# Eight of the 24 gates of each mixer by seven block products ahead of the attention, and the sink as a column of the summed row

## The chip, the cores and the metric

The kernel runs on one core of a Trainium2 chip, in one launch. The metric is the device time in microseconds (us). Three runs of the kernel before gave 2394.09, 2394.22 and 2396.0 us. A core has engines that run their own instruction lists and wait for each other by semaphores: TensorE (PE, matrix products into PSUM banks), VectorE (DVE), ScalarE (ACT), GpSimd (POOL), and SyncE (SP), which here only issues DMAs. ScalarE and POOL issue DMAs too. A DMA's issue waits in the list of the engine that issues it.

## The reference

A trunk of two layers over 512 tokens of width 1024, in float32. Each layer is a half-step feed-forward, a mixer, and a second half-step feed-forward. The mixer is what changes:

```python
h = rms_norm(x, norm_g[l, 1])
proj = h @ w_in[l]
qa, ka, va, qd, kd, vd, qc, kc, vc = jnp.split(proj, PROJ_OFFSETS, axis=-1)
...
g = jax.nn.sigmoid(h @ w_gate[l] + b_gate[l]).reshape(B, S, N_BRANCHES, D_MODEL)
merged = (g[:, :, 0] * (ya @ w_branch[l, 0])
          + g[:, :, 1] * (yb @ w_branch[l, 1])
          + g[:, :, 2] * (yc @ w_branch[l, 2]))
x = x + merged @ w_o[l]
```

Here `ya` is the neighbourhood attention (8 heads on a grid of 8 x 64 tokens), `yb` the differential attention (4 heads with two softmax maps each) and `yc` the windowed attention (8 query heads, 2 key heads). So there are three gates of width 1024. In tiles of 128 output columns they are 24 gates, named (branch, tile): (0, 0) to (2, 7). In the windowed attention the softmax has one more logit, the sink of its head, which has no value behind it:

```python
sink_l = jnp.broadcast_to(sink.astype(jnp.float32).reshape(Hkv, G, 1, 1), logits.shape[:-1] + (1,))
p = jax.nn.softmax(jnp.concatenate([logits, sink_l], axis=-1), axis=-1)[..., :-1]
```

## The kernel before

Activations lie transposed: eight tiles `h` of 128 features by 512 tokens. A float32 product is made of three products of reduced operands: each matrix is split into a high part (a cast on ScalarE, `whi`, line 100) and a low part (a subtraction on VectorE, `wlo`, line 101), and TensorE sums hi x hi, hi x lo and lo x hi (lines 122, 123 and 125). A **direct gate** is one weight tile of 1024 columns: 8 x 3 = 24 matmuls of 512 columns, then a multiplication by the norm (`z`, line 1583) and a tanh on ScalarE. The results stay in SBUF until the merge of their branch.

The feed-forward has another way, class `Seven` (its matmuls are on line 889). It takes two output tiles at a time, as a 2 x 2 block product in seven block products instead of eight, by sums and differences of the blocks. The activations' sums are class `Sides`, made once per feed-forward (VectorE lines 699 to 709 and the low halves on line 720). The weights' sums are made by DMAs that add, partly in DRAM long before. A tile of Seven needs several split weights: `wa` (the first raw tile), `w31` (a sum loaded as `wsum`), `w24`, and the corner `w22` from `a22`. A stage that is not prepared in DRAM uses the order `WIDE_FIRST` with 72 matmuls a tile, 12 of 512 columns and 60 of 256.

In the mixer, `qk(0)` computes the first queries and keys, and `v_stacked` (lines 1276, 1277 and 1280) the values of the neighbourhood attention: four weight tiles, each with 24 matmuls of 512, into four PSUM banks that stay open until the last weight. The banks are emptied by `vn` on ScalarE (line 1302) and VectorE (line 1303). The three attentions then run as generators. `beside(attention, steps, n)` sets a list of other products (queries, keys, gates, merges) between the eight steps of each attention stage, so that TensorE has work while a softmax is under way. There are four stages of each attention: na, diff and gqa.

Raw weights come by SP's queue into `raw`, three buffers: a load is issued when the buffer's last reader is done, and SP's loads go out in their order. `ahead_by` (line 789) issues a few of the DMAs that prepare the next feed-forward after each weight, as many as `PACE` says.

The sink in the windowed attention: the row of 256 or 384 scores is lifted by its bias on VectorE, which also gives the row's bound `negm`; ScalarE makes the exponentials and their sum `tot`; one more exponential of a single column gives the sink's share `se` (line 1571), which VectorE adds to `tot` (line 1572).

## Time and profile before

| | before |
|---|---|
| three runs, us | 2394.09, 2394.22, 2396.0 |
| the profiled execution's own time, us | 2394.87 |
| its span on the core, us | 2393.1 |
| mixer 0, from its first q product to the output product, us of the span | about 352 to 865 |
| mixer 1 stands behind mixer 0 by, us | 1181.1 |

The span leaves out what lies around the core's first and last instruction, 1.8 us here. All times of instructions are counted from the span's start. In the group rows "out<-in" names the tiles without their numbers, and "x24" is a count of instructions. In the chain of work that ended last each piece stands with its start and length; in the timeline a bracket at the end says how long the engine stood idle before the instruction, and who released it.

### The profile page before, as it was taken

How to read it: one execution, taken by the hardware profiler on the slowest of the kernel's cores; microseconds unless marked ns; L12 is line 12 of the kernel's file. 1: busy time of each engine (PE TensorE's matmuls, PEld its weight loads, DVE VectorE, ACT ScalarE, POOL GpSimd, SP SyncE). 2: the span in 40 equal slices, each digit the busy share in tenths (PEclk: the TensorE clock that was granted, in tenths of full speed). 3: DMA queues.
4: the chain of work that ended last, by engine and by line, in shares of the span. 5: the costliest groups of instructions: out<-in, count | busy, mean ns of one | idle time of the engine just before them, and what ended most of it. 6: DMA issues, size and time to landing. Idle time of an engine off the chain costs nothing.

```text
span 2393.1 us, 35725 instructions
## 1 busy us (share of the span) xinstructions
PE 2377.4 (99%) x12954; PEld 2047.3 (86%) x12954; DVE 1834.6 (77%) x3328; ACT 1380.0 (58%) x2551; POOL 369.3 (15%) x524
## 2 busy tenths in 40 slices
PE   9999999999999999999999999999999999999998
PEld 7999888888888888888888888888888888888887
DVE  6999885766667679997899997767666666899832
ACT  5565545756566446664456664467566574566632
POOL 3100024412131100110201011333212100000000
PEclk9999999999999999999999999999999999999999
DMA  7665787655698647886858887766556624455532
GB/s 200 182 185 163 248 243 211 172 157 136 193 221 250 190 147 232 266 257 200 233 185 240 272 268 234 215 170 167 144 140 168 157 95 132 163 190 189 172 114 71
DMA packets 149776, 452.92 MB, mean 189 GB/s; under 512 B 18264, under 2 KB 23688, under 8 KB 148640
## 3 DMA queue, kind: packets, MB, share of 16 engines
q1 hardware_dynamic: 89856, 278.50, 34.5%
q0 software_dynamic: 40352, 107.36, 22.6%
q10 hardware_dynamic: 19392, 64.78, 7.5%
q8 instruction: 102, 1.67, 0.3%
q14 instruction: 74, 0.61, 0.1%
HBM read 428.52 MB, written 138.44 MB: 237 GB/s over the span
## 4 chain that ended last, share of the span: by engine, by line
PE 95%; DVE 2%; ACT 1%; issue 1%; DMA 1%; SPq 0%; POOLq 0%; POOL 0%; ACTq 0%; DVEq 0%
PE mm L889 18%; PE plain L395 10%; PE mm L125 9%; PE pr L889 9%; PE mm L123 9%; PE mm L122 9%; PE pv L889 4%; PE mm L395 3%; PE av L1382 2%; PE mm L1600 2%; PE mm L1595 2%; PE mm L1596 2%; PE t L1372 1%; PE s L1327 1%; PE s L1328 1%; PE av L1484 1%
## 5 line engine op out<-in xcount | busy, mean ns | idle before, releaser
L101 DVE TENSOR_TENSOR wlo<-raw,whi 128x1024 fp32r<-128x1024 f32 x234 | 278.8, 1196 | 111.5 <-ACT whi L100 91.0
L100 ACT CAST whi<-raw 128x1024 fp32r<-128x1024 f32 x234 | 238.6, 1027 | 211.3 <-PE mm L123 76.6
L122 PE MATMUL mm<-h,whi 128*128 128x512 f32 x800 | 318.7, 398 | 0.0
L123 PE MATMUL mm<-h,whi 128*128 128x512 f32 x800 | 313.7, 392 | 0.0
L125 PE MATMUL mm<-h,wlo 128*128 128x512 f32 x800 | 197.8, 389 | 0.6 <-DVE wlo L101 0.6
L109 DVE TENSOR_TENSOR wlo<-raw,whi 128x1024 fp32r<-128x1024 f32 x156 | 184.2, 1218 | 6.0 <-ACT whi L108 5.9
L125 PEld LDWEIGHTS mm<-h,wlo 128*128 128x128 f32 x800 | 150.1, 188 | 32.3 <-DVE wlo L101 1.0
L123 PEld LDWEIGHTS mm<-h,whi 128*128 128x128 f32 x800 | 150.5, 188 | 28.8
L122 PEld LDWEIGHTS mm<-h,whi 128*128 128x128 f32 x800 | 150.4, 188 | 28.4
L108 ACT CAST whi<-raw 128x1024 fp32r<-128x1024 f32 x156 | 156.8, 1051 | 10.2 <-DMA raw<-in_w_gu 8.6
L395 PE MATMUL plain<-g,whi 128*128 128x512 f32 x672 | 160.7, 389 | 0.0
L395 PEld LDWEIGHTS plain<-g,whi 128*128 128x128 f32 x672 | 126.1, 188 | 26.3
L761 POOL DMA_DIRECT2D d_odd<-in_w_gu x60 | 51.6, 859 | 516.1 <-DVE gu L925 254.6
L1341 ACT ACTIVATE lg<-lg,negm 128x256 f32<-128x256 f32 (+1 forms) x192 | 114.0, 594 | 29.0 <-DVE negm L1338 23.2
L1009 ACT COPY gu<-mm 128x512 f32<-128x512 f32 (+1 forms) x78 | 41.9, 538 | 131.2 <-PE mm L889 131.2
L108 ACT CAST whi<-wsum 128x1024 fp32r<-128x1024 f32 x90 | 94.8, 1053 | 39.3 <-PE pv L889 32.7
L109 DVE TENSOR_TENSOR wlo<-wsum,whi 128x1024 fp32r<-128x1024 f32 x90 | 109.5, 1217 | 5.5 <-PE plain L395 3.2
L925 DVE TENSOR_TENSOR gu<-pr,gu 128x256 f32<-128x256 f32 x234 | 98.2, 420 | 8.6 <-ACT gu L963 4.4
L1583 DVE TENSOR_TENSOR z<-mm,rb 128x512 f32<-128x512 f32 x48 | 33.2, 691 | 81.7 <-PE mm L125 81.6
L889 PEld LDWEIGHTS mm<-h,whi 128*128 128x128 f32 x624 | 83.7, 189 | 5.6 <-PE st L250 0.4
L1222 DVE SCALAR_TENSOR_TENSOR qn<-mm,rb 128x512 f32<-128x512 f32 x44 | 34.8, 794 | 68.1 <-PE mm L125 68.1
L889 PE MATMUL mm<-h,whi 128*128 128x256 f32 x624 | 86.9, 281 | 0.0
(367 smaller groups left out, 6185.3 us busy)
## 6 DMA issues: line engine op xcount, KB each, us to landing
raw<-in_w_gu SPq DMA_DIRECT2D x94, 512.0 KB, 4.4
d_odd<-in_w_gu ACTq DMA_DIRECT2D x60, 512.0 KB, 7.2
d_even<-in_w_gu ACTq DMA_DIRECT2D x60, 512.0 KB, 6.0
d_odd<-in_w_gu POOLq DMA_DIRECT2D x60, 512.0 KB, 8.4
wsum<-d_odd SPq DMA_DIRECT2D x60, 512.0 KB, 3.6
raw<-d_even SPq DMA_DIRECT2D x60, 512.0 KB, 4.6
raw<-in_w_gate SPq DMA_DIRECT2D x48, 512.0 KB, 5.0
raw<-in_w_qk SPq DMA_DIRECT2D x44, 512.0 KB, 3.9
```

The source lines that it names most:

```text
L100: nc.scalar.copy(hi[:, w], raw[:, w])
L101: lower[:] = [nc.vector.tensor_tensor(out=lo[:, w], in0=raw[:, w], in1=f(hi[:, w]), op=ALU.subtract).ins]
L108: nc.scalar.copy(hi, src)
L109: nc.vector.tensor_tensor(out=lo, in0=src, in1=f(hi), op=ALU.subtract)
L122: nc.tensor.matmul(ps, wh, xhi[k], start=k == 0, stop=False)
L123: nc.tensor.matmul(ps, wh, xlo[k], start=False, stop=False)
L125: nc.tensor.matmul(ps, wl, xhi[k], start=False, stop=k == n - 1)
L395: nc.tensor.matmul(ps, w, x, start=start, stop=stop, skip_group_check=True)
L761: dma = nc.gpsimd.dma_start(out, more, accum_op=ALU.add, max_dma_last_dim=4 * 1024)
L889: nc.tensor.matmul(out, wk, bk, start=go, stop=end, skip_group_check=True)
L925: nc.vector.tensor_tensor(out=out, in0=in0, in1=in1, op=ALU.add)
L1341: nc.scalar.activation(p, p, AF.Exp, bias=negm, scale=-1.0, accum_out=total)
```

## The change

In each mixer eight gates, (0, 2) to (0, 7), (1, 0) and (1, 1), are computed as four tiles of a new class `Gates`, which is `Seven` with another source, other buffers and another end. The four tiles run between `v_stacked` and the first attention stage. Their sides (class `MixedSides`) are made while `v_stacked` runs, one after each of its weights. A result goes through its tanh and is stored to DRAM from POOL's queue; the merge that needs it loads it again on SP's queue. The gates (1, 2) to (1, 7) are still direct products beside the attention, and they go to DRAM and back too, from their `z` buffer. The gates (0, 0), (0, 1) and those of branch 2 stay as they were, in SBUF.

The lists beside the attention lose the eight gates. The four na stages and the second diff stage have as many products as before; diff 0, 1 and 3 and gqa 0, 2 and 3 have one fewer, gqa 1 two fewer. `PACE["mixer"]` is raised, as there are fewer weights to pace by. In the windowed attention POOL copies the sink's negative into the column behind the row of scores, and the one exponential sums that column too; `se` and its addition are gone.

```diff
-    "mixer": ((1, 1, 2.5), (0.6, 1, 1.8)),
+    "mixer": ((1.2, 2, 2.5), (0.7, 1.4, 1.8)),
...
+    AHEAD = ((0, 1), (0, 2), (0, 3), (1, 0))
+
+    class MixedSides(Sides):
+        def whole_room(self, mp):
+            return mp.tile([P, S], F32, tag="gate", name="xf", bufs=3)
...
+        def kept(self, mp, one, t3):
+            self.t = [mp.tile([P, 2, H], F32R, tag="yp", name="side", bufs=12) for _ in range(3)]
+            for src, out in zip((one[:, 0], one[:, 1], t3), self.t):
+                self.halves(src, out)
...
+    class Gates(Seven):
...
+        def total(self, m):
+            t = self.fp.tile([P, 2, S], F32, tag="pt", name="wsum", bufs=4)
+            nc.sync.dma_start(t, self.source(m).rearrange("n p c -> p n c")[:, :, 0:S])
+            t = t.rearrange("p n c -> p (n c)")
+            nc.gpsimd.dma_start(t, self.source(m)[1], accum_op=ALU.add)
+            return t
+        def scratch(self):
+            return self.fp.tile([P, 5, H], F32, tag="pt", name="gu", bufs=4)
...
+            def opened(t, odd):
+                c = i * KC + 2 * n + odd
+                nc.scalar.activation(t, t, AF.Tanh, bias=self.bg[:, c : c + 1], scale=0.5)
+                self.stored(i, 2 * n + odd, t)
...
-                        p = l_tile()[:, :w]
-                        softmax(p, ps, reversed_view(bias, 383 - u, [[1, w]]), nsink[:, head : head + 1], negm[:, j : j + 1], tot[:, j : j + 1])
-                        se = small.tile([P, 1], F32, tag="se", name="se")
-                        nc.scalar.activation(se, negm[:, j : j + 1], AF.Exp, bias=sink[:, head : head + 1])
-                        nc.vector.tensor_tensor(out=tot[:, j : j + 1], in0=tot[:, j : j + 1], in1=se, op=ALU.add)
+                        full = l_tile()
+                        p = full[:, :w]
+                        nc.gpsimd.tensor_copy(out=full[:, w : w + 1], in_=nsink[:, head : head + 1])
+                        softmax(p, ps, reversed_view(bias, 383 - u, [[1, w]]), nsink[:, head : head + 1], negm[:, j : j + 1], tot[:, j : j + 1], full[:, : w + 1])
...
+            def stored(i, m, t):
+                gates[i, m] = dram.tile([P, S], F32, tag=f"d_gate{l}{i}{m}", name="d_gate")
+                nc.gpsimd.dma_start(gates[i, m], t)
...
+                if i < 2 and (i, mm) != (0, 0):
+                    for m in (2 * mm, 2 * mm + 1):
+                        if mm % 2:
+                            t = work.tile([P, S], F32, tag="x", name="gate", bufs=2)
+                        else:
+                            t = mp.tile([P, S], F32, tag="gate", name="gate", bufs=3)
+                        nc.sync.dma_start(t, gates[i, m])
...
-            run([qk(0), v_stacked()])
-            beside(attend_na(0), [qk(1), *g0(0)], 3)
+            outset = (x for g in (qk(0), v_stacked()) for x in g)
+            sides = []
+            next(outset)
+            for c in range(4):
+                next(outset)
+                sides.append(MixedSides(mp, h, c, [None] * KC))
+            run([outset])
+            tiles = Gates(l, h, mp, sides, bg, stored)
+            tiles.fetch(0)
+            tiles.wa[0] = parted(tiles.raw[0])
+            tiles.fetch_a22(0)
+            tiles.fetch(1)
+            with tc.issue_after(sides[3].mark):
+                tiles.w31[0] = parted(tiles.sums[0])
+            for m in range(tiles.end):
+                tiles.tile(m)
+            with tiles.in_order():
+                tiles.flush()
+            beside(attend_na(0), [qk(1), gate(0, 0)], 3)
...
-            beside(attend_gqa(2), [merge(1, 3), *[gate(2, m, "v", 8) for m in range(3)]], 4)
-            beside(attend_gqa(3), [gate(2, 3, "v", 8), *[gate(2, m) for m in (4, 5)]], 3)
+            beside(attend_gqa(2), [merge(1, 3), *opened(2, 3)], 3)
+            beside(attend_gqa(3), opened(4, 5), 2)
```

How the change moves instructions is shown at three places of mixer 0. The first is TensorE at the end of `v_stacked` (`av` is its fourth bank, `mm_3941` and `mm_3952` its first), before:

```order
L1276 MATMUL av_3944<-whi_4039,h7_3835 128x512
L1277 MATMUL av_3944<-whi_4039,h7_3835 128x512
L1280 MATMUL av_3944<-wlo_4040,h6_3793 128x512
L1280 MATMUL av_3944<-wlo_4040,h7_3835 128x512
L122 MATMUL mm_4102<-h0_3239,whi_4096 128x512
L123 MATMUL mm_4102<-h0_3239,whi_4096 128x512
```

and with the change, where lines 1390, 1391 and 1394 are `v_stacked`, line 921 is a tile of Gates, `whi_4168` and `wlo_4169` are wa, and `whi_4179` is w31:

```order
L1391 MATMUL av_3955<-whi_4107,h7_3835 128x512
L1394 MATMUL av_3955<-wlo_4108,h6_3793 128x512
L1394 MATMUL av_3955<-wlo_4108,h7_3835 128x512
L921 MATMUL mm_4184<-h0_3239,whi_4168 128x256 x2
L921 MATMUL mm_4184<-h1_3252,whi_4168 128x256 x2
L921 MATMUL mm_4184<-h2_3431,whi_4168 128x256 x2
L921 MATMUL mm_4184<-h3_3444,whi_4168 128x256 x2
L921 MATMUL mm_4184<-h0_3239,wlo_4169 128x256
L921 MATMUL mm_4184<-h1_3252,wlo_4169 128x256
L921 MATMUL mm_4184<-h2_3431,wlo_4169 128x256
L921 MATMUL mm_4184<-h3_3444,wlo_4169 128x256
L921 MATMUL pr_4185<-side_3943,whi_4179 128x512
```

Where the second query product followed, the first tile of Gates does; its bank `mm_4184` is the one that `mm_3952` held. The second place is VectorE where it empties that bank. Before, the two rows on `mm_3941` stand right behind the low parts of three weights of queries and gates:

```order
L1230 TENSOR_TENSOR qk_3938<-qn_3933,qk_3938 64x512
L101 TENSOR_TENSOR wlo_4097<-raw_4095,whi_4096 128x1024
L101 TENSOR_TENSOR wlo_4171<-raw_4169,whi_4170 128x1024
L101 TENSOR_TENSOR wlo_4257<-raw_4255,whi_4256 128x1024
L1303 SCALAR_TENSOR_TENSOR vn_4053<-mm_3941,rs_3878,vn_4053 128x4x64
L1303 SCALAR_TENSOR_TENSOR vn_4056<-mm_3941,rs_3878,vn_4056 128x4x64
```

and with the change (line 732 the low halves of the last side, `wlo_4108` the fourth v weight, `wlo_4180` w31, line 915 the sums for w24, `wlo_4188` w24):

```order
L732 TENSOR_TENSOR side_4099<-tsum_4092,side_4099 128x256
L101 TENSOR_TENSOR wlo_4108<-raw_4106,whi_4107 128x1024
L109 TENSOR_TENSOR wlo_4169<-raw_4166,whi_4168 128x1024
L109 TENSOR_TENSOR wlo_4180<-wsum_4163,whi_4179 128x1024
L915 TENSOR_TENSOR raw_4166<-wsum_4163,raw_4166 128x512
L915 TENSOR_TENSOR raw_4166<-raw_4166 128x512
L1417 SCALAR_TENSOR_TENSOR vn_4121<-mm_3952,rs_3870,vn_4121 128x4x64
L109 TENSOR_TENSOR wlo_4188<-raw_4166,whi_4187 128x1024
L1417 SCALAR_TENSOR_TENSOR vn_4124<-mm_3952,rs_3870,vn_4124 128x4x64
```

The second row that empties the bank now stands behind all the sides and three weights of the first tile. The third place is ScalarE at the casts of the first queries and keys, before:

```order
L199 COPY rb_3917<-st_3912 128x512
L1229 CAST qk_3921<-qn_3919 64x512
L1229 CAST qk_3924<-qn_3919 64x512
L100 CAST whi_4096<-raw_4095 128x1024
L1229 CAST qk_3935<-qn_3933 64x512
L1229 CAST qk_3938<-qn_3933 64x512
```

and with the change:

```order
L1343 CAST qk_3913<-qn_3911 64x512
L1343 CAST qk_3916<-qn_3911 64x512
L108 CAST whi_4168<-raw_4166 128x1024
L1343 CAST qk_3927<-qn_3925 64x512
L1343 CAST qk_3930<-qn_3925 64x512
L731 CAST side_4047<-tsum_4041 128x256
L731 CAST side_4048<-tsum_4041 128x256
```

Between the two pairs of casts the weight of the second query product stood; now wa stands there, and the casts of the third side follow. On SP's queue the load of wa (`raw_4166`) stands behind the four v weights, the loads of three weight sums and a row of biases.

More of the change, by code (lines that the diff above doesn't have):

```diff
@@ L703, in __init__ @@
             b11, b12, b21, b22 = t[0][:, :H], t[0][:, H:], t[1][:, :H], t[1][:, H:]
-            one, other = [fp.tile([P, 2, H], F32, tag="g", name="tsum", bufs=gbufs[0]) for _ in range(2)]
+            one, other = self.sum_rooms(fp)
             t1, t2, t3, t4 = one[:, 0], one[:, 1], other[:, 0], other[:, 1]
@@ L709, in __init__, with whole_room, sum_rooms, kept @@
             nc.vector.scalar_tensor_tensor(out=t4, in0=t2, scalar=-1.0, in1=b21, op0=ALU.mult, op1=ALU.subtract)
+            self.b11, self.b21, self.b22 = h.both[e][:, :, :H], h.both[o][:, :, :H], h.both[o][:, :, H:]
+            self.t4, self.b12 = t4, h.both[e][:, :, H:]
+            self.kept(fp, one, t3)
+        def whole_room(self, fp):
+            return fp.tile([P, S], F32, tag="g", name="xf", bufs=gbufs[0])
+        def sum_rooms(self, fp):
+            return [fp.tile([P, 2, H], F32, tag="g", name="tsum", bufs=gbufs[0]) for _ in range(2)]
+        def kept(self, fp, one, t3):
             two = fp.tile([P, 2, S], F32R, tag="pair", name="pair", bufs=4)
@@ L966, in tile @@
                 rest()
-                w22 = [fp.tile([P, S], F32R, tag=t, name=t) for t in ("w22h", "w22l")]
+                w22 = self.corner()
                 a22 = self.a22.pop(m)
@@ L998, in tile, with sum22, fourth, corner_sum @@
             u3 = self.halves(1, 6, 7)
-            fold = folded[0] and m < FOLD
+            def sum22():
+                nc.scalar.copy(g[:, 2 : 2 + u3], one[:, 0:u3])
+                for n in range(u3):
+                    add(q[4], q[4], q[2 + n])
+            def fourth():
+                self.product(4, one, blocks(w22), side(4), stop=True)
+            def corner_sum():
+                n = self.halves(1, 4, 6, 7)
+                nc.scalar.copy(q[3], one[:, n - 1])
+                if n == 2:
+                    add(q[3], one[:, 0], q[3])
+            self.tail = self.closing(m, g, sum22, fourth, corner_sum)
+        def closing(self, m, g, sum22, fourth, corner_sum):
+            fp, fold = self.fp, folded[0] and m < FOLD
+            gn, un = [g[:, n : n + 2].rearrange("p a c -> p (a c)") for n in (0, 3)]
             hi, lo, to = None, None, un
@@ new lines, in encoder, with __init__, source, total @@
+    class Gates(Seven):
+        def __init__(self, l, h, mp, sides, bg, stored):
+            super().__init__("gates", l, h, mp, sides, [], [])
+            self.layer, self.bg, self.stored, self.end = l, bg, stored, len(AHEAD)
+        def source(self, m):
+            i, n = AHEAD[m]
+            return a["w_gate"][self.layer, i, 2 * n : 2 * n + 2]
+        def total(self, m):
+            t = self.fp.tile([P, 2, S], F32, tag="pt", name="wsum", bufs=4)
[3 more added lines that the diff above has]
+            return t
+        def scratch(self):
+            return self.fp.tile([P, 5, H], F32, tag="pt", name="gu", bufs=4)
+        def corner(self):
+            return [self.fp.tile([P, S], F32R, tag=t, name=t) for t in ("m4", "m5")]
+        def closing(self, m, g, sum22, fourth, corner_sum):
+            i, n = AHEAD[m]
+            one, two = [g[:, c : c + 2].rearrange("p a c -> p (a c)") for c in (0, 3)]
+            def opened(t, odd):
+                c = i * KC + 2 * n + odd
+                nc.scalar.activation(t, t, AF.Tanh, bias=self.bg[:, c : c + 1], scale=0.5)
+                self.stored(i, 2 * n + odd, t)
+            def first():
+                opened(one, 0)
+            def second():
+                corner_sum()
+                nc.vector.scalar_tensor_tensor(out=two, in0=two, scalar=-1.0, in1=self.h.rb, op0=ALU.mult, op1=ALU.mult)
+            def third():
+                opened(two, 1)
+            return sum22, first, fourth, second, third
@@ L1334, in l_tile, with softmax @@
                 return mp.tile([P, S], F32, tag="lg", name="lg", bufs=5)
-            def softmax(p, ps, bias, first, negm, total):
+            def softmax(p, ps, bias, first, negm, total, row=None):
                 nc.vector.tensor_tensor_reduce(
@@ L1340, in softmax @@
                 )
-                nc.scalar.activation(p, p, AF.Exp, bias=negm, scale=-1.0, accum_out=total)
+                row = p if row is None else row
+                nc.scalar.activation(row, row, AF.Exp, bias=negm, scale=-1.0, accum_out=total)
             def t_tile():
@@ L1638, in gqa_queries @@
                 yield
-            merged = [mp.tile([P, S], F32, tag=f"m{m}", name=f"m{m}") for m in range(KC)]
             mh, ml = [None] * KC, [None] * KC
@@ new lines, in mixer @@
+            tiles.fetch_a22(0)
[6 more added lines that the diff above has]
+                tiles.flush()
+            merged = [mp.tile([P, S], F32, tag=f"m{m}", name=f"m{m}") for m in range(KC)]
+            beside(attend_na(0), [qk(1), gate(0, 0)], 3)
+            beside(attend_na(1), [qk(2), gate(0, 1)], 3)
```

92 lines of the change are left out of this document (48 added, 44 removed).

## The prediction

> **What bounds the kernel now.** I read the page first (busy shares, slices, the chain that ended last), then the chain in order of time, then busy time by stretch, then single rows of the engines around the place that the change touches.
>
> ```profile
> span 2393.1 us, 35725 instructions
> PE 2377.4 (99%) x12954; PEld 2047.3 (86%) x12954; DVE 1834.6 (77%) x3328; ACT 1380.0 (58%) x2551; POOL 369.3 (15%) x524
> PE 95%; DVE 2%; ACT 1%; issue 1%; DMA 1%; SPq 0%; POOLq 0%; POOL 0%; ACTq 0%; DVEq 0%
> ```
>
> TensorE is busy 99% of the span, and it holds 95% of the chain. So a matmul that goes is worth its pitch, and a wait that appears in front of TensorE costs its whole length. By stretch (columns: us, busy time of each engine with instructions, PE clock, DMA share, GB/s):
>
> ```profile
> 352.40:364.60 12.20, 12.20 (x62) 10.20 (x60) 6.53 (x9) 5.14 (x6) 2.54 (x2) 1.00 0.69 237
> 364.60:386.30 21.70, 21.70 (x98) 17.93 (x97) 11.26 (x15) 8.34 (x14) 11.63 (x15) 1.00 0.87 231
> 732.30:761.30 29.00, 29.00 (x152) 24.84 (x151) 21.67 (x54) 20.78 (x50) 4.11 (x5) 1.00 0.89 253
> ```
>
> The rows are the first q and k products of mixer 0, v_stacked, and the third stage of the windowed attention. TensorE has no gap in any of them and runs at its full granted clock (1.00). In v_stacked VectorE has 10.4 us of 21.7 free, but the DMA engines are busy 87%.
>
> **What the change takes from TensorE.** Durations come from the chain in order of time (start, us, engine, tile, line): one tile of seven products in the first feed-forward, and the eight low matmuls of a direct product in mixer 0.
>
> ```profile
> 153.76 2.87 PE mm L889 x24
> 156.63 1.40 PE pr L889 x8
> ...
> 163.70 2.87 PE mm L889 x24
> 390.24 1.81 PE mm L125 x8
> ```
>
> The tile repeats after 163.70 - 153.76 = 9.94 us: 12 matmuls of 512 columns and 60 of 256. A direct gate is 24 matmuls of 512, 24 x 1.81 / 8 = 5.43 us, and two are 10.86. One tile saves 0.92 us, four tiles a mixer and two mixers 8 x 0.92 = **7.4 us**, 0.31% of the time. The two shapes run here at 0.226 us (512) and about 0.118 us (256: 1.40 us for four of 512 and four of 256).
>
> The Trainium skill, "TensorE: Matmul & The Clock Gate", section "Back-to-back issue gap", speaks against the change: it says that in a stream of weight loads and matmuls the smaller matmul pays more per column, about 81 ns at 128 columns and 131 ns at 512. By an estimate between its two figures (some 98 ns at 256) a tile would take 12 x 131 + 60 x 98 ns = 7.5 us against 6.3 us for two gates, and eight tiles would lose 9 us. The rows above, 0.226 and 0.118 us, do not agree with it, so I keep 7.4 us.
>
> **What the change adds ahead of the tiles.** The sides are built on VectorE between the parts of v_stacked. VectorE's rows, of v_stacked in mixer 0 and of the same side work in a feed-forward (start, us):
>
> ```profile
> 356.24 2.36 DVE L101 TENSOR_TENSOR wlo<-raw,whi 128x1024 fp32r<-128x1024 f32 x2
> 365.61 1.28 DVE L1222 SCALAR_TENSOR_TENSOR qn<-mm,rb 128x512 f32<-128x512 f32 x2
> 370.16 1.41 DVE L1230 TENSOR_TENSOR qk<-qn,qk 64x512 fp32r<-64x512 f32 x2 [1.30 <-ACT qk L1229]
> 384.16 0.88 DVE L1303 SCALAR_TENSOR_TENSOR vn<-mm,rs,vn 128x256 fp32r<-128x256 f32 x2 [0.54 <-ACT vn L1302]
> 1209.80 1.28 DVE L699 TENSOR_TENSOR xf<-h 128x512 f32<-128x512 f32 x2
> 1211.00 0.42 DVE L706 TENSOR_TENSOR tsum<-xf 128x256 f32<-128x256 f32 x1
> 1211.33 0.42 DVE L708 TENSOR_TENSOR tsum<-xf 128x256 f32<-128x256 f32 x1
> 1212.01 0.68 DVE L699 TENSOR_TENSOR xf<-h 128x512 f32<-128x512 f32 x1
> 1213.88 0.68 DVE L699 TENSOR_TENSOR xf<-h 128x512 f32<-128x512 f32 x1
> 386.16 0.45 PE av L1280 x2
> ```
>
> A side takes 1213.88 - 1209.80 = 4.08 us less 0.60 for the next side's xf that stands inside, 3.48 us; with its third half cut in two, 3.55 us. VectorE's list from 356.24 us to the second vn, which empties the PSUM bank that the first Gates product writes, is: four v weights and three weights of tile 0 (wa, w31, w24), 7 x 1.18 = 8.3; four sides 14.2; qn 1.3; qk 2.8; two sums at 0.68, 1.4; two vn 0.9. Together 28.9 us, to 385.1 us. TensorE ends v_stacked at 386.16 + 0.45 = 386.6 us. If VectorE never waited, the tiles would start on time with 1.5 us over. But it waits, for loads:
>
> ```profile
> raw<-in_w_gate SPq DMA_DIRECT2D x2, 512.0 KB, 9.0
> raw<-in_w_va SPq DMA_DIRECT2D x2, 512.0 KB, 4.5
> d_x<-gu POOLq DMA_DIRECT2D x1, 256.0 KB, 2.6
> d_x<-gu POOLq DMA_DIRECT2D x1, 256.0 KB, 6.0
> 354.40 0.57 POOL L73 DMA_DIRECT2D d_x<-gu  x1 [7.47 <-DVE gu L398]
> 1535.49 0.57 POOL L73 DMA_DIRECT2D d_x<-gu  x1 [4.81 <-DVE gu L398]
> 368.56 1.05 ACT L100 CAST whi<-raw 128x1024 fp32r<-128x1024 f32 x1 [0.96 <-ACT qk L1229]
> 369.52 1.25 ACT L1229 CAST qk<-qn 64x512 fp32r<-64x512 f32 x2
> 357.99 0.79 PE st L206 x8
> 1539.08 0.79 PE st L206 x8
> ```
>
> The first four rows are DMA issues (KB each, median us to landing) in 364 to 392, 350 to 364, 350 to 364 and 1526 to 1546 us. **The load of wa** takes the raw buffer of the second v weight, so it is issued only when that weight's low part is done: 356.24 + 1.18 (first v) + 3.55 (side 0) + 1.2 + 5 x 0.34 (most of side 1, a piece of 256 columns every 0.34 us) + 1.18 = 365.1 us. ScalarE casts wa ahead of the casts of k, so k's low parts and everything after them on VectorE stand behind the landing. From the landing: cast 1.05, half of the qk casts 0.63, then on VectorE two qk 1.4, five pieces of side 2 1.7, two v weights 2.4, side 3 3.55, three tile weights 3.5, sums 1.4, vn 0.9: 16.5 us. To be done by 386.6 us the load must land by 370.1 us, 5.0 us after its issue. The v loads before it took 4.5 us, the gate loads of the same stretch 9.0. Three sums (a load and an accumulating DMA of 512 KB each) are now queued ahead of it, in a stretch that is 0.69 to 0.87 busy. So the stall in mixer 0 lies between 0 (4.5 us to land) and 4.0 us (9.0); between ends so far apart I take the middle, 6.75 us, **1.8 us**: the slower rows are nearer in place, the quicker ones nearer in time.
>
> In **mixer 1**, 1539.08 - 357.99 = 1181.1 us later, side 0 must wait for the last store of x out of the memory that it takes over. That store landed at 1535.49 + 6.0, in mixer 0's clock 360.4 us; in mixer 0 it landed at 354.40 + 2.6 = 357.0 us, without harm. From 360.4 us the list of VectorE to the second v weight is 3.55 + 2.9 + 1.18 = 7.6 us, the load goes out at 368.0 us, and the stall is 2.4 (4.5 us to land) to 6.9 us (9.0). If the store is as early as in mixer 0, it is 0 to 4.0 us. I take the middle of the late case, **4.7 us**, since the store's row shows it late.
>
> **What else it adds or takes.** At the opening of another stage of such tiles TensorE waited once:
>
> ```profile
> 1232.75 1.19 PE L889 MATMUL mm<-pair,whi 128*128 128x512 f32 x4 [0.16 <-ACT gu L957]
> 157.93 0.36 ACT L957 COPY gu<-mm 128x256 f32<-128x256 f32 x1
> 160.34 0.69 DVE L1024 SCALAR_TENSOR_TENSOR gu<-gu 128x512 f32<-128x512 f32 x1
> L1571 ACT ACTIVATE se<-negm,sink x64: 277/280/290, 652.2 to 1962.3; 128x1 f32<-128x1 f32 x64
> ```
>
> - Opening of the tiles, one wait of 0.16 us or a few: I take 0.3 us a mixer (up to 0.7).
> - A result of tile 0 leaves 160.34 + 0.69 - 153.76 = 7.3 us into tile 1 plus its tanh, 7.9. Tile 2 first writes the same buffer 9.94 + 157.93 - 153.76 = 14.1 us into tile 1. The store has 6.2 us to land; the two stores of that size above took 2.6 and 6.0. I take nothing; a store of 8 us on POOL's queue would cost 2 us a mixer.
> - The sink: 64 ScalarE instructions of 0.280 us and as many small VectorE ones go. Neither engine was waited for there (29.00 us of TensorE beside 21.67 and 20.78), so nothing is gained. The new copies stand on POOL, 4.11 of 29 us busy; a copy late behind one of POOL's own DMA waits would delay an Exp. Five score buffers lie between: I take nothing, 0 to 4 us.
> - Fewer gates beside the attention: the third windowed stage loses one of its three, so 29.0 - 5.4 = 23.6 us of TensorE against at most 21.67 - 1.2 = 20.5 on VectorE. TensorE stays longest. Stores and reloads of 14 gates a mixer are 7 MB, in stretches with free DMA time except this one. I take nothing.
>
> **Sum.** -7.4 + 1.8 + 4.7 + 0.6 = -0.3 us. Against the profiled execution (2394.87 us, its span 2393.1) that is 2394.6; that execution lay 0.65 above the median of the three (2394.22), so I say **2393.9 us**.
>
> **The rivals.**
> 1. *The outset hides it.* The loads land within 5 us and the store of x early, and only openings remain: -7.4 + 0.6 = -6.8, **2387.4 us**. For it: in a feed-forward opening VectorE worked 21.62 of 22.00 us and TensorE lost nothing:
> ```profile
> 1200.00:1222.00 22.00, 22.00 (x110) 18.53 (x109) 21.62 (x43) 10.03 (x17) 1.20 (x1) 1.00 0.47 166
> 2072.00:2092.00 20.00, 19.34 (x116) 16.52 (x115) 19.62 (x36) 13.51 (x23) 0.00 (x0) 1.00 0.63 214
> ```
> Against it: the DMA share there is 0.47; in the next such opening, at 0.63, 0.66 us were lost, and here it is 0.87.
> 2. *Slower: the load of wa lands late in both mixers.* With 10 us to land, one more than the nearest rows since the sums go ahead of it, and the long openings: -7.4 + 5.0 + 7.9 + 1.4 = +6.9, **2401.1 us**; with the store waits of 2 us a mixer, 2405. My middle is near break-even and each us of a late load lands on TensorE whole, so it is slower by over 0.2% once the two loads together are some 5 us later than I take them.
> 3. *Too little beside the attention, or Exp behind POOL.* up to 4 us on my forecast, 2398; on a late load it adds to rival 2.
> 4. *Rules of the Trainium skill.* VectorE is held whenever POOL reads SBUF. The mask additions on POOL stood beside a weight's low part:
> ```profile
> 364.62 3.69 POOL L1411 TENSOR_TENSOR nab<-mask,rp 128x256 f32<-128x256 f32 x3 [3.60 <-DMA rp<-in_na_rpb]
> 364.47 1.23 DVE L101 TENSOR_TENSOR wlo<-raw,whi 128x1024 fp32r<-128x1024 f32 x1 [4.36 <-PE mm L125]
> ```
> 1.23 us, no hold. If there were one, 3.69 us twice a mixer would land on a full VectorE: +14.8 on my forecast, 2408.7. The rule is in "SBUF — State Buffer", section "SBUF: two separate sides" (one port pair, locked for a whole instruction, for a VectorE operation with two SBUF inputs against a GpSimd one that reads SBUF); the trace does not agree. The matmul rule above, by the estimate there, would give +9 in place of -7.4, 2410.3.
>
> **Chances.** Forecast and what lies around it 0.43; rival 1 0.31; rival 2 0.19; rival 3 0.04; rule cases 0.03. The measurement can tell 0.2% (4.8 us) from no change: faster (below 2389.4) 0.31, same 0.45 (half of rival 3 with the forecast), slower (above 2399.0) 0.24. Range 2386.5 to 2402: rival 1 to the larger part of rival 2. The forecast's own is 2390 to 2398.
>
> **What would show it.** Gates tiles 9.94 us apart on TensorE; gaps of TensorE between the last matmul of v_stacked and the first of tile 0, released by VectorE's vn, about 2 us in mixer 0 and 5 us in mixer 1; VectorE near full from 356 us on; the load of wa issued near 365 us, landing near 372. No gap there, or wa landed by 370, means rival 1; ScalarE idle for wa past 374, rival 2; gaps in the windowed stages, rival 3. I am wrong too if the tiles' pitch is over 10.4 us.

## The result, and the profile after

The changed kernel takes 2409.5 us (median of 6 runs, 2408.89 to 2411.21) against 2394.15 us (6 runs) before: a ratio of 1.0066, 95% interval 1.0053 to 1.0079. It is **slower by 15 us**, above the predicted range. From the page after, then TensorE's waits after (for whom; us in total, times, longest):

```profile
span 2409.0 us, 36581 instructions
PE 2377.7 (99%) x13146; PEld 2051.4 (85%) x13146; DVE 1906.1 (79%) x3424; ACT 1401.6 (58%) x2575; POOL 407.7 (17%) x624
PE 88%; DVE 4%; issue 3%; ACT 2%; DMA 2%; POOL 1%; POOLq 0%; SPq 0%; ACTq 0%; DVEq 0%
PE mm L1394 <- DVE wlo L101: 7.1, 3, 4.3
PE t L1487 <- DVE pl L1490: 3.2, 2, 2.1
PE mm L921 <- DVE vn L1417: 2.9, 2, 2.2
```

TensorE's share of the chain fell from 95% to 88%. Its busy time did not fall at all, though it has less to do; most of the reason is below. Line 1394 is `v_stacked` on the low parts of its weights: the largest wait is inside `v_stacked`, not at the first tile. The tiles themselves cost what was counted. In the chain in order of time, mixer 0:

```profile
411.95 2.87 PE mm L921 x24
...
421.89 2.87 PE mm L921 x24
```

421.89 - 411.95 = 9.94 us, as in the feed-forward. So the saving is there, and more than that is lost elsewhere. Busy time by stretch: `v_stacked`, then all up to the first scores, then the attention with what stands beside it, for mixer 0 and mixer 1. The kernel before:

```profile
364.60:386.60 22.00, 22.00 (x99) 18.19 (x98) 11.42 (x15) 8.63 (x14) 11.63 (x15) 1.00 0.87 232
386.60:391.90 5.30, 5.30 (x26) 4.37 (x25) 2.49 (x4) 2.95 (x5) 0.00 (x0) 1.00 0.87 239
391.90:815.40 423.50, 422.64 (x2221) 358.10 (x2220) 292.19 (x631) 270.43 (x575) 104.06 (x146) 1.00 0.71 189
1545.70:1567.90 22.20, 22.20 (x99) 18.13 (x98) 11.96 (x15) 8.28 (x13) 10.63 (x14) 1.00 0.77 201
1567.90:1573.20 5.30, 5.30 (x25) 4.38 (x24) 2.50 (x4) 3.20 (x5) 0.00 (x0) 1.00 0.52 191
1573.20:1997.00 423.80, 422.93 (x2222) 358.05 (x2221) 291.39 (x632) 270.95 (x576) 87.68 (x125) 1.00 0.54 142
```

and the changed kernel:

```profile
362.40:392.70 30.30, 25.55 (x99) 19.85 (x96) 25.07 (x37) 10.10 (x20) 11.51 (x15) 0.89 0.85 209
392.70:440.00 47.30, 46.00 (x314) 42.12 (x313) 40.14 (x67) 30.60 (x55) 4.75 (x8) 1.00 0.56 182
440.00:823.80 383.80, 379.55 (x2030) 321.49 (x2029) 274.01 (x583) 249.59 (x528) 119.53 (x192) 1.00 0.84 220
1553.00:1579.90 26.90, 22.91 (x98) 17.64 (x96) 20.76 (x37) 10.05 (x19) 15.43 (x12) 1.00 0.64 158
1579.90:1630.10 50.20, 47.43 (x314) 43.37 (x314) 41.34 (x67) 31.96 (x58) 5.32 (x9) 0.97 0.59 187
1630.10:2012.50 382.40, 380.00 (x2029) 321.79 (x2028) 275.41 (x583) 251.66 (x529) 94.80 (x163) 1.00 0.58 154
```

The second stretch should be 5.3 us plus four tiles at 9.94, 45.1 us; the third should be shorter by eight gates at 5.43 us, 43.4 us. What is over is lost:

| lost, us | mixer 0 | mixer 1 |
|---|---|---|
| `v_stacked` | 30.3 - 22.0 = 8.3 | 26.9 - 22.2 = 4.7 |
| to the first scores | 47.3 - 45.1 = 2.2 | 50.2 - 45.1 = 5.1 |
| attention | 383.8 - (423.5 - 43.4) = 3.7 | 382.4 - (423.8 - 43.4) = 2.0 |
| sum | 14.2 | 11.8 |
| less the saving of four tiles | 10.5 | 8.1 |

That makes 18.6 us. The span grew by 15.9; the rest of the program was 2.7 us shorter in this execution, most of it a wait of 2.1 us at the very start that before's had.

Where the largest loss comes from is read on four engines, around 364 to 389 us after (the row's bracket: idle time before, and who ended it). ScalarE, VectorE, POOL and TensorE:

```profile
373.60 1.05 ACT L108 CAST whi<-raw 128x1024 fp32r<-128x1024 f32 x1 [6.74 <-DMA raw<-in_w_gate]
374.55 1.25 ACT L1343 CAST qk<-qn 64x512 fp32r<-64x512 f32 x2
375.20 1.40 DVE L1344 TENSOR_TENSOR qk<-qn,qk 64x512 fp32r<-64x512 f32 x2 [4.19 <-ACT qk L1343]
377.31 3.10 DVE L709 SCALAR_TENSOR_TENSOR tsum<-tsum,xf 128x256 f32<-128x256 f32 x1
381.00 1.21 DVE L101 TENSOR_TENSOR wlo<-raw,whi 128x1024 fp32r<-128x1024 f32 x1
377.64 2.48 POOL L1526 TENSOR_TENSOR nab<-mask,rp 128x256 f32<-128x256 f32 x3
382.27 1.65 PE L1394 MATMUL mm<-wlo,h 128*128 128x512 f32 x3 [4.30 <-DVE wlo L101]
```

ScalarE stands 6.74 us for wa, which it has no use for yet, with k's casts behind it. VectorE then stands 4.19 us for those casts, with the rest of side 2 and the third v weight behind them. When it goes on, one operation of side 2 that takes 0.41 us elsewhere takes 3.10 us, just while POOL adds the attention's masks. TensorE gets its low part 4.30 us late. The load of wa was issued at 364.4 us and took 9.1 us; in mixer 1 it took 9.2 us, and ScalarE stood 6.47 us for it in the same way. Behind such waits TensorE also runs at half its clock for a while:

```profile
380.00:390.00 10.00, 7.73 (x21) 6.11 (x22) 9.97 (x18) 2.54 (x5) 0.93 (x2) 0.66 0.75 183
382.30:388.50 6.20, 6.20 (x15) 4.85 (x16) 6.20 (x12) 2.06 (x4) 0.81 (x1) 0.50 0.69 161
1582.00:1588.00 6.00, 5.92 (x33) 5.57 (x34) 3.35 (x8) 3.31 (x8) 0.00 (x0) 0.72 0.65 211
```

For 6.2 us after the wait the granted clock is 0.50: 3.1 us of TensorE's work more. In mixer 1 a clock of 0.72 over 6 us makes 1.7 us more, after three waits of 1.1 to 2.2 us within 12 us. Together that is 4.8 us. TensorE's busy time rose by 0.3 us where it should have fallen by 7.4, so this is the greater part of the reason; the other 2.9 us were not followed up.

Which of these engines held the first tile back is told by the chain of work that ended last. For mixer 0 and then for mixer 1, some of its pieces up to the first tile of Gates:

```profile
363.23 1.15 DVE wlo L101
364.43 9.07 DMA raw<-in_w_gate
377.40 3.02 DVE tsum L709
392.90 0.41 DVE vn L1417
393.45 1.66 PE mm L921 x12
1554.48 9.15 DMA raw<-in_w_gate
1581.53 0.41 DVE vn L1417
1582.08 2.04 PE mm L921 x12
```

In mixer 0 the chain runs over the load of wa, ScalarE and then VectorE's list to the second `vn` (for 3.38 us it names another gate's load, beside which VectorE was busy with the last side). TensorE does not stand in it between 363 us and the first tile. So by this chain TensorE's wait of 4.30 us inside `v_stacked` is no loss of its own: without it TensorE would have waited longer for the first tile's bank, which VectorE freed at 393.3 us. The half clock of mixer 0 was hidden in the same way, since TensorE still waited 0.70 us for that bank. The half clock of mixer 1 fell behind the start of the first tile (1582.08 us), where nothing hid it.

### The profile page after: what moved, and what is told of

It is laid out like the page before. It is cut to its first block, busy times and chain, and to the rows that moved or that the text cites. A ratio compares the mean times of both kernels' runs of the same rounds, so it can differ in the third digit from the quotient of the medians.

```text
span 2409.0 us, 36581 instructions
## 1 busy us (share of the span) xinstructions
PE 2377.7 (99%) x13146; PEld 2051.4 (85%) x13146; DVE 1906.1 (79%) x3424; ACT 1401.6 (58%) x2575; POOL 407.7 (17%) x624
## 4 chain that ended last, share of the span: by engine, by line
PE 88%; DVE 4%; issue 3%; ACT 2%; DMA 2%; POOL 1%; POOLq 0%; SPq 0%; ACTq 0%; DVEq 0%
PE mm L921 19%; PE plain L395 11%; PE pr L921 9%; PE mm L125 7%; PE mm L123 6%; PE mm L122 6%; PE pv L921 5%; PE mm L395 4%; PE mm L1730 2%; PE av L1497 2%; PE mm L1726 2%; PE mm L1725 2%; PE t L1487 1%; PE s L1441 1%; PE s L1442 1%
## 5 line engine op out<-in xcount | busy, mean ns | idle before, releaser
L122 PE MATMUL mm<-h,whi 128*128 128x512 f32 x672 | 268.4, 399 | 0.0
L123 PE MATMUL mm<-h,whi 128*128 128x512 f32 x672 | 264.7, 394 | 0.0
L125 PE MATMUL mm<-h,wlo 128*128 128x512 f32 x672 | 167.0, 390 | 0.3 <-DVE wlo L101 0.3
L125 PEld LDWEIGHTS mm<-h,wlo 128*128 128x128 f32 x672 | 125.9, 188 | 26.9 <-DVE wlo L101 0.8
L123 PEld LDWEIGHTS mm<-h,whi 128*128 128x128 f32 x672 | 126.5, 188 | 23.3
L122 PEld LDWEIGHTS mm<-h,whi 128*128 128x128 f32 x672 | 126.4, 188 | 22.7
L1456 ACT ACTIVATE lg<-lg,negm 128x256 f32<-128x256 f32 (+2 forms) x192 | 114.3, 596 | 20.1 <-DVE negm L1452 17.0
L109 DVE TENSOR_TENSOR wlo<-wsum,whi 128x1024 fp32r<-128x1024 f32 x98 | 119.2, 1216 | 5.1 <-PE plain L395 2.5
L957 DVE TENSOR_TENSOR gu<-pr,gu 128x256 f32<-128x256 f32 x258 | 108.2, 419 | 9.7 <-ACT gu L995 5.4
L921 PE MATMUL mm<-side,whi 128*128 128x256 f32 (+1 forms) x512 | 103.9, 335 | 0.9 <-ACT gu L989 0.9
L921 PEld LDWEIGHTS mm<-h,whi 128*128 128x128 f32 x688 | 91.9, 189 | 9.3 <-issue 2.6
L921 PE MATMUL mm<-h,whi 128*128 128x256 f32 x688 | 96.0, 281 | 2.9 <-DVE vn L1417 2.9
L921 PE MATMUL pv<-h,whi 128*128 128x512 f32 (+1 forms) x448 | 94.7, 343 | 0.0
```

Of the source, the lines that this page charges most:

```text
L109: nc.vector.tensor_tensor(out=lo, in0=src, in1=f(hi), op=ALU.subtract)
L122: nc.tensor.matmul(ps, wh, xhi[k], start=k == 0, stop=False)
L123: nc.tensor.matmul(ps, wh, xlo[k], start=False, stop=False)
L125: nc.tensor.matmul(ps, wl, xhi[k], start=False, stop=k == n - 1)
L921: nc.tensor.matmul(out, wk, bk, start=go, stop=end, skip_group_check=True)
L957: nc.vector.tensor_tensor(out=out, in0=in0, in1=in1, op=ALU.add)
```

## The experiments

Theory A: engines that stand in order behind a late load (first of all wa's) make the loss. Theory B: VectorE has too much to do ahead of the tiles, in whatever order. Theory C: POOL's mask additions hold VectorE. Times are medians, and each ratio is to runs of the kernel before on the same chip.

**The order on ScalarE, the mask additions, the sink.** `late_wa`:

```diff
-            tiles.wa[0] = parted(tiles.raw[0])
             tiles.fetch_a22(0)
             tiles.fetch(1)
             with tc.issue_after(sides[3].mark):
+                tiles.wa[0] = parted(tiles.raw[0])
                 tiles.w31[0] = parted(tiles.sums[0])
```

> The changed kernel, but ScalarE's cast of wa stands behind the casts of all four sides and of k, so that nothing of v_stacked stands behind wa's load. Theory A (the load of wa lands 9 us after its issue, and ScalarE and then VectorE stand still behind it): VectorE's idle time of 4.2 and 5.0 us at the casts of k goes, TensorE's waits for the low parts of the v weights (4.3, 1.1, 1.7 us) go, and with the first also the half clock behind it (about 3 us): 2396 to 2401 us. Theory B (VectorE has too much to do in the stretch, whatever the order): the same waits come back before the first tile, 2406 to 2410 us. Theory C (POOL's mask additions hold VectorE): 2403 to 2407 us, with one VectorE row of about 3 us left beside them.

`late_nab` makes the mask additions for the first two heads wait for `v_stacked`'s last `vn`; `late_both` does both:

```diff
+                        if pair == 0:
+                            tc.add_manual_dep(added_bias.ins, emptied[0].name, WAIT, reason="quiet")
```

> The changed kernel, but POOL's mask additions for the first two heads wait until v_stacked's banks are emptied. Theory A (the late load of wa is what counts): VectorE still idles 4 to 5 us for it; the 3.10 us row of a 0.41 us subtraction in mixer 0 is gone, so 2.7 us less there and part of the half clock: 2404 to 2408 us. Theory C (POOL holds VectorE): 2400 to 2404 us. Theory B (too much work on VectorE): 2407 to 2410 us.

> Both moves at once: cast of wa behind the sides, mask additions behind v_stacked. Theory A: little under the first move alone, 2395 to 2400 us. Theory C: clearly under it, by 3 us or more. Theory B: 2404 to 2409 us. If all stalls ahead of the tiles were gone, the other losses (attention stages, about 3.8 and 2.1 us, and the openings) would leave about 2393 us.

`sink_alone` is the kernel before with only the sink's edit:

> The kernel before with only the sink moved into the summed row (one POOL copy a step in place of an exponential and an addition). All theories: 2393 to 2396 us, no difference. If POOL's copy delays the exponentials, the windowed stages lengthen and it is 2396 to 2400 us.

| run | us | ratio to before (95%) |
|---|---|---|
| late_wa | 2403.4 | 1.0036 (1.0023 to 1.0050) |
| late_nab | 2415.9 | 1.0090 (1.0075 to 1.0105) |
| late_both | 2407.2 | 1.0054 (1.0037 to 1.0071) |
| sink_alone | 2398.0 | 1.0019 (1.0010 to 1.0029) |

`late_wa` gives back some 5 us with one line (it is some 10 us over its own runs of the kernel before, the change 15.4): TensorE's waits inside `v_stacked` for the v weights are gone in mixer 0, and the half clock with them. Its time lies above the range for theory A and inside the one for theory C. What is left in mixer 0 is the opening of the tiles:

```profile
388.75 1.19 PE L921 MATMUL mm<-h,whi 128*128 128x256 f32 x8 [1.64 <-DVE vn L1417]
401.54 0.74 PE L921 MATMUL pr<-side,wlo 128*128 128x256 f32 x4 [1.60 <-DVE wlo L109]
```

In mixer 1 theory C's sign is there: beside POOL's mask additions one VectorE operation on a side takes 2.73 us in place of 0.42, and TensorE then waits 2.17 us for the bank (VectorE and POOL):

```profile
1561.87 2.73 DVE L732 TENSOR_TENSOR side<-tsum,side 128x256 fp32r<-128x256 f32 x1
1562.07 2.25 POOL L1526 TENSOR_TENSOR nab<-mask,rp 128x256 f32<-128x256 f32 x3
```

`late_nab` is slower than every theory said, and `late_both` lies in the range for theory B. But the medians of these two do not price theory C, since moving the additions does two things. They now stand in POOL's list ahead of the stores of the gates, and the third tile waits for a store. ScalarE in `late_both`:

```profile
415.69 0.37 ACT L989 COPY gu<-mm 128x256 f32<-128x256 f32 x1 [2.60 <-DMA d_gate<-gu]
```

This is the store wait of 2 us that the prediction named; it came only when the queue in front of the stores was lengthened. The two effects come apart when the time from the start of `v_stacked` is cut at the first tile. What each profiled execution loses in mixer 0 and mixer 1, against 22.0 and 22.2 us for `v_stacked`, 45.1 us from the first tile to the first scores, and 10.9 us for the two direct gates where a run has them (the last three runs follow below):

| run | up to the first tile, us | from there to the first scores, us |
|---|---|---|
| the change | 9.1, 6.9 | 1.5, 2.9 |
| late_wa | 2.6, 5.2 | 2.9, 2.0 |
| late_both | 0.6, 1.8 | 6.7, 4.4 |
| sums_late | 4.0, 1.6 | 1.5, 2.0 |
| late3 | 1.2, 1.5 | 3.2, 2.2 |
| order3 | -0.1, 1.6 | 2.5, 1.4 |

Up to the first tile A takes 8.2 of 16.0 us, and with the additions out of the way another 5.4 go, so C has a price. What is won by it is lost again behind the first tile, much of it to the store waits (1.98 us in mixer 0, 1.33 in mixer 1) and, in mixer 0, to 1.7 us at half clock behind them. What is left for B there is some 2.4 us. These are single executions, and moving one thing shifts the others, so the shares are rough.

`sink_alone` was 4.6 us slower than before, in the range for late exponentials. But its mixers were as long as before's; the feed-forwards were longer. The edit removes six buffers of one column from a pool, and with them every later tile moves by 192 bytes a partition; the change's wider `pad` (88 columns for 40) makes up for just that, and my kernel did not have it. The next two runs separate it.

**The pad, the gates without the sink, and two direct gates ahead of the tiles.** `sink_pad` adds `pad` 88 to `sink_alone`; `pad_alone` is the kernel before with `pad` 88; `gates_alone` is the change without the sink's edit (and `pad` 40). `fill2` is `late_wa` with two gates moved from the differential stages:

```diff
             run([outset])
+            run(away(3, 4))
```

> The kernel before with only the sink moved into the summed row, and the pad of 40 columns widened to 88 as in the change (the sink's six little buffers are gone, the pad takes their place, so that all later tiles keep their addresses). In the run without the wider pad the mixers were as long as before and the 4.6 us more lay in the feed-forwards. Theory of addresses: 2392 to 2395 us, no difference to before. Theory of POOL's copy: 2397 to 2399 us again.

> The kernel before with only the pad widened from 40 to 88 columns: nothing computed changes, every tile behind it moves by 192 bytes a partition. Theory of addresses: slower than before by 2 to 6 us. Otherwise no difference, 2392 to 2395 us.

> The changed kernel with the sink as it was before (and the pad of 40 columns). All of the loss lies in the gates by my reading of the two traces (v_stacked 8.3 and 4.7 us longer, tiles 2.1 and 5.1 us over their own time, attention stages 3.8 and 2.1 us): 2407 to 2411 us. If the sink has a share: 2403 to 2406 us.

> The cast of wa behind the sides, as in the earlier run, and two direct gates, (1, 3) and (1, 4), moved from the differential stages to between v_stacked and the first tile: 10.9 us of TensorE with only 3.8 us of VectorE. If what is left of the loss is VectorE's backlog at the opening of the tiles (2403.4 us in the earlier run, with 1.8, 1.8, 0.6 us of waits there in mixer 0 and 0.6, 2.3, 0.9, 0.6 in mixer 1), these waits go and it is 2394 to 2398 us. If the backlog only moves on behind the two gates, or the differential stages lose as much for want of work, 2401 to 2404 us.

| run | us | ratio to before (95%) |
|---|---|---|
| sink_pad | 2393.7 | 0.9997 (0.9988 to 1.0006) |
| pad_alone | 2398.6 | 1.0020 (1.0011 to 1.0030) |
| gates_alone | 2405.8 | 1.0050 (1.0035 to 1.0065) |
| fill2 | 2415.6 | 1.0092 (1.0075 to 1.0109) |

The sink by itself costs nothing, as predicted; an address shift alone costs 4.4 us. It shows in the feed-forward's plain products, before and in `pad_alone` (us in total, mean ns of one):

```profile
L395 PE MATMUL plain<-g,whi 128*128 128x512 f32 x672 | 160.7, 389 | 0.0
L395 PE MATMUL plain<-g,whi 128*128 128x512 f32 x672 | 165.1, 395 | 0.0
```

The gates alone are slow, so most of the loss is theirs. Their time lies in the range given for a share of the sink, but whether the sink adds to the loss in their company is not settled, as the intervals of `gates_alone` and of the change overlap.

`fill2` missed badly and told most. Its tiles opened with 0.6 us of waits only, so VectorE does catch up beside the two direct gates. But ScalarE again had a cast of a gate's weight ahead of k's casts, now that of the first direct gate, and `v_stacked` took 30.9 and 32.9 us:

```profile
373.77 1.05 ACT L100 CAST whi<-raw 128x1024 fp32r<-128x1024 f32 x1 [6.69 <-DMA raw<-in_w_gate]
375.37 1.41 DVE L1344 TENSOR_TENSOR qk<-qn,qk 64x512 fp32r<-64x512 f32 x2 [3.97 <-ACT qk L1343]
```

**The lists put in order, step by step.** `fill2_guard` puts the two direct gates' casts behind the sides' casts; `fill2_order` puts all weights after the first direct gate behind the emptying of `v_stacked`'s first bank on ScalarE. The second, against `fill2`:

```diff
+            guard[:] = [emptied[1], sides[3].mark]
             run(away(3, 4))
...
-            with tc.issue_after(sides[3].mark):
+            with tc.issue_after(emptied[1]):
                 tiles.wa[0] = parted(tiles.raw[0])
```

> As the run with two direct gates ahead of the tiles (2415.6 us), but the casts of these gates' weights stand behind the casts of the sides too. In that run ScalarE again stood 6.7 and 6.5 us behind a gate's load, now the first direct gate's, ahead of k's casts, while the tiles opened with 0.6 us of waits only. If the order of ScalarE's list behind a late load is the cause (theory A), v_stacked is 23 to 25 us long again, the tiles still open well, and it is 2393 to 2398 us. If VectorE's amount of work is the cause (theory B), the waits move to the direct gates, 2402 to 2408 us.

> As the run above, and the weights behind the first direct gate are cast behind the emptying of v_stacked's first bank, so that the bank comes free ahead of three low parts of 1.2 us each on VectorE. Theory A: 1 to 3 us under the run above, 2391 to 2396 us; the floor, were no wait left, is 2394 - 7.4 = 2387 us. Theory B: no difference to the run above.

They gave 2422.7 (1.0116, 1.0099 to 1.0133) and 2408.8 us (1.0059, 1.0043 to 1.0076); both expectations of A were missed, and the first is slower than B said too. `v_stacked` was short again in mixer 0 (23.8 and 23.7 us) but not in mixer 1 (26.4 and 28.1 us), and TensorE stood 11.0 us (`fill2_guard`) and 3.9 us (`fill2_order`) ahead of a direct gate in mixer 0. The cause stood in SyncE's list. In `fill2_order`, with POOL:

```profile
372.64 13.31 SPq L1518 DMA_DIRECT2D rp<-in_na_rpb  x2
386.09 0.50 SPq L98 DMA_DIRECT2D raw<-in_w_gate  x1
378.72 6.67 POOL L1528 TENSOR_TENSOR nab<-mask,rp 128x256 f32<-128x256 f32 x3 [0.39 <-DMA rp<-in_na_rpb]
```

A row of biases for the attention far ahead, whose only buffer is still in use, held the queue until 386 us, with the gate's weight behind it. What used the buffer were POOL's mask additions, to which SyncE's wait is put down: three of them took 6.67 us beside a busy VectorE, one alone 5.19, where the shortest take 0.77. So this late load too comes from POOL and VectorE in each other's way. `order3` puts these rows behind the load of wa, and the fourth v weight's cast behind those of sides 0 and 1; `late3` does the same without the direct gates:

```diff
+                    with tc.issue_after(first_load[0]):
+                        nc.sync.dma_start(
...
+            guard[:] = [sides[1].mark]
             run([outset])
```

> As the run with two direct gates and the bank emptied early (2408.8 us), with two more moves in the engines' lists: on SyncE the loads of the attention's bias rows stand behind the load of wa (in that run one of them stood in the queue until 385 us and the weight of the second direct gate behind it, so that ScalarE waited 8.6 us); on ScalarE the cast of the fourth v weight stands behind the casts of sides 0 and 1 (VectorE waited 2.0 us for one of them). If engines standing in order behind late loads are the whole cause (theory A): TensorE's waits of 4.1 and 2.9 us ahead of the second direct gate go, and most of the 1.5 and 4.3 us ahead of k's bank: 2391 to 2398 us. If VectorE has too much to do (theory B): they come back elsewhere ahead of the tiles, 2402 to 2408 us.

> The same two moves on the changed kernel with the cast of wa behind the sides (2403.4 us), without direct gates ahead of the tiles. Theory A: 2397 to 2401 us. Theory B: 2401 to 2404 us, with the waits at the opening of the tiles (1.8, 1.8, 0.6 and 2.3, 0.9, 0.6 us) as they were, since only the two direct gates give VectorE time to catch up.

`order3` takes 2396.6 us (1.0012, 1.0002 to 1.0022) and `late3` 2398.4 us (1.0020, 1.0010 to 1.0029). `v_stacked` in `order3`, both mixers:

```profile
363.40:385.50 22.10, 22.10 (x100) 18.24 (x98) 19.21 (x36) 10.41 (x21) 6.44 (x9) 1.00 1.05 265
1545.90:1569.80 23.90, 22.39 (x99) 18.18 (x98) 21.02 (x41) 11.21 (x22) 6.50 (x9) 1.00 1.05 290
```

VectorE is busy 19.2 us of `v_stacked`'s 22.1, and TensorE loses nothing there in mixer 0. Each against the kernel before on its own chip, the change is 15.4 us slower and `order3` 3.3, so some 12 of the 15 us go by reorderings and two moved gates, with no work taken away. Both are in the ranges for theory A. They do not rule out C, though: with the bias rows late, POOL's mask additions start at 390.5 us in `order3`, behind `v_stacked`, so that VectorE is not held there.

**The sums ahead of wa.** `sums_late` leaves ScalarE's order as in the change, and puts the weight sums of tiles 1 and 2 and the bias rows behind the load of wa; `order4` does that to `order3`.

```diff
-            tiles.fetch(1)
+            with tc.issue_after(first_load[0]):
+                tiles.fetch(1)
```

> The changed kernel with ScalarE's order untouched (wa is still cast ahead of k's casts), but on SyncE the weight sums of the second and third tile and the attention's bias rows stand behind the load of wa, so that 1.5 MB of loads and as much of accumulating DMAs no longer go ahead of it. If these loads are why wa took 9.1 us, it lands 4.5 to 6 us after its issue, ScalarE's idle time of 6.7 and 6.5 us shrinks to 2 to 4 us, and it is 2399 to 2404 us. If the DMA engines are full without them, or the queue is not the reason, wa takes 8 to 9 us again and it is 2407 to 2411 us.

> The run with two direct gates and the three lists put in order (2396.6 us), with the weight sums of the second and third tile behind the load of wa as well. If queued sums still cost time there (d_x landing late in mixer 1 aside), 2391 to 2395 us. If the sums now come too late for tiles 1 and 2, TensorE waits there and it is 2398 us or more. No difference, 2395 to 2398 us, if the loads were no longer on the path.

`sums_late` takes 2399.6 us (1.0030, 1.0018 to 1.0041). The load of wa landed 6.6 us after its issue in mixer 0 and 5.2 us in mixer 1; ScalarE, both mixers:

```profile
372.13 1.05 ACT L108 CAST whi<-raw 128x1024 fp32r<-128x1024 f32 x1 [4.28 <-DMA raw<-in_w_gate]
1555.00 1.05 ACT L108 CAST whi<-raw 128x1024 fp32r<-128x1024 f32 x1 [2.58 <-DMA raw<-in_w_gate]
```

So the late landing came largely from what was queued ahead of it. But the landing is not the whole gain: up to the first tile of mixer 0 the run loses 4.0 us in place of 9.1, and 2.5 us of that are the landing; 2.7 us are VectorE's held operation, which takes its usual time here, as the bias rows and with them POOL's additions come later. `order4` takes 2397.8 us (1.0013, 1.0004 to 1.0022), as `order3`: with the casts in order the load is no longer on the path. No version beats the kernel before.

## Why the prediction was wrong

- **The saving** was sized right: 9.94 us a tile, 7.4 us in all. The Trainium skill's lower figures for a stream of matmuls, quoted in the prediction, do not hold here.
- **The mechanism** was the one named: the load of wa, ScalarE's cast of it ahead of k's casts, VectorE behind both, and the first tile's bank last. Rival 2 was right in kind. The step that failed is the size of the stall, the terms that were summed up to that bank. Counted from the first matmul of `v_stacked`, with the measured values from the chain after:

| term, us | mixer 0 predicted | measured | mixer 1 predicted | measured |
|---|---|---|---|---|
| wa's load is issued after | 0.5 | 2.0 | 3.4 | 1.5 |
| it lands within | 6.75 | 9.1 | 6.75 | 9.2 |
| from the landing to the emptied bank | 16.5 | 19.8 | 16.5 | 18.3 |
| less `v_stacked` itself | 22.0 | 22.0 | 22.0 | 22.2 |
| stall | 1.8 | 8.9 | 4.7 | 6.8 |

  First of these, the middle between 4.5 and 9.0 us for the landing: it took 9.1 and 9.2 us, the price of the nearest rows of the same stretch, and `sums_late` (6.6 and 5.2 us) shows that the queued sums and bias rows belonged in the sum as more than a remark. With 9.0 us the prediction's own terms gave -7.4 + 4.0 + 6.9 + 0.6 = +4.1, some 2398.3. The second is the list behind the landing, 3.3 and 1.8 us too short: in mixer 0, 2.7 us of that are the operation held beside POOL's additions.
- **The late store** of x in mixer 1 did not cost what I took. VectorE stood 1.52 us for it, but wa's load went out 1.5 us after the start of `v_stacked`, no later than in mixer 0. That `v_stacked` of mixer 1 grew by just the 4.7 us forecast for the stall is luck: its terms were wrong in opposite directions, and 2.2 us more of the stall showed at the first tile.
- **The place** where the wait shows was wrong. I reckoned from the landing to the bank of the first tile only. The third v weight's low part stands in the same list, and TensorE wants it some six microseconds earlier (at 378.0 us in mixer 0, where its wait begins; the first tile would have been wanted near 384.4), inside `v_stacked`. So of the gaps that I named ahead of the first tile only 0.70 and 2.17 us were to be seen. This alone adds nothing to the time, as the chain shows.
- **Half clock** was in no term: 3.1 us of TensorE's work in mixer 0, hidden behind VectorE, and 1.7 us in mixer 1 that were not hidden. The Trainium skill, "TensorE: Matmul & The Clock Gate", section "What's actually happening", says that the array falls to half its clock after an idle window of about 3.4 us and is back after a busy one. The trace agrees in part: by the rows above the half clock lasted some 6.8 us in mixer 0 (10 us at 0.66) and 3.4 us in mixer 1 (6 us at 0.72), two and one such windows. But the three waits of mixer 1 were shorter than a window each.
- **The rule on POOL and VectorE** was dismissed on a misread row. There POOL's additions were the ones held (3.69 us for three, 2.48 in the row after the change), and VectorE's instruction was not. The 3.10 us row shows the hold from the other side, and in mixer 1 three additions took 9.82 us beside a busy VectorE (POOL, after):

```profile
1570.63 9.82 POOL L1526 TENSOR_TENSOR nab<-mask,rp 128x256 f32<-128x256 f32 x3 [5.32 <-DMA rp<-in_na_rpb]
```

  The Trainium skill, "SBUF — State Buffer", section "SBUF: two separate sides", states this lock (whichever of the two starts first holds it for its whole instruction). The trace agrees that one shuts out the other for whole instructions; who will be held can't be read from the recorded starts, as the 3.10 us row starts at 377.31 us, ahead of POOL's additions at 377.64. My price for it, 14.8 us, was wrong as well: on the chain it is 2.7 us in mixer 0 of the change, and by `late_wa` and `late_both` some 5 us for both mixers. That the two cases of the skill's rules came to 2408.7 and 2410.3 us, next to the 2409.5 measured, is luck: the tiles kept their 9.94 us, and the hold made only a part of the loss.
- **The opening of the tiles** at 0.3 us a mixer was too small: from the first tile to the first scores 1.5 and 2.9 us went, the latter with the 1.7 us at half clock. Backlog on VectorE is not the reason for the rest, since 1.3 us a mixer remain in `fill2`, where 10.9 us of direct products ahead of the tiles let it catch up.
- **The attention**, at nothing, lost 3.7 and 2.0 us. Part is VectorE's list beside POOL's additions: in mixer 1 a pair of low parts of q and k took 3.15 us in place of 1.40, and the `pl` behind it, by way of ScalarE's exponentials, came 1.13 us late for TensorE (VectorE, POOL and TensorE, after):

```profile
1639.12 3.15 DVE L1344 TENSOR_TENSOR qk<-qn,qk 64x512 fp32r<-64x512 f32 x2
1638.44 2.55 POOL L1526 TENSOR_TENSOR nab<-mask,rp 128x256 f32<-128x256 f32 x3
1645.00 0.41 PE L1487 MATMUL t<-ident,lg 128*128 128x128 f32 x2 [1.13 <-DVE pl L1490]
```

  Near the first windowed stage of mixer 0 TensorE waited 2.06 us for another `pl` (at 706.67 us); what made it late is not explained, and `gates_alone`, `fill2` and `order3` have no such wait there.
- **The sink** at nothing was right for the sink by itself (`sink_pad`); beside the gates it is not settled. The stores of 2 us at nothing were right for the change as it was made.
- Rival 1's evidence, a feed-forward opening with VectorE 98% busy and TensorE unhurt, did not carry over. There VectorE was idle for 0.38 of 22.00 us, so its list waited for next to nothing; here it stood 4.19 and 5.01 us for k's casts. In `order3` VectorE was busy 19.2 of 22.1 us and TensorE unhurt as well.

## What to carry to other kernels

Work that is added to a full stretch must be checked list by list: what stands *behind* each instruction that waits for a load, on each engine and on each DMA queue, matters more than the sum of busy times. A load for later must not have its first reader in an engine's list ahead of work for now, and a load into a single busy buffer must not stand in a queue ahead of weights. Take the landing time of a load from the nearest rows of the same stretch, and make it longer by what is newly queued ahead. Where work for POOL and work for VectorE on SBUF meet in a full stretch, add the time that one of them is held. And read a loss from the chain that ended last before pricing a wait: TensorE's longest wait here was not a loss of its own.
